# Decoder block with product-key experts on one core: every second weight block split by GpSimd, fewer activation pairs in routing and gate grid, and gate rows laid out with the routing

## The chip, the cores and the metric

One core of a Trainium2 chip runs the whole program. The metric is the device time of one execution in microseconds (us). Besides TensorE (matmul, PE in the profile, with PEld for its weight loads), VectorE (DVE), ScalarE (ACT) and GpSimd (POOL), the core has SyncE (SP), whose queue issues most of the loads. The profile shows TensorE's granted clock, where 1.00 is 2.4 GHz and 0.50 is 1.2 GHz.

## The reference, cut to what matters

The input x has 256 tokens of 1024 columns. A first half of the block (two attention branches, merged by gates) gives a new x. Then comes the expert layer, around which everything here turns:

```
h2 = modulate(rms_norm(x, g_ffn), sh2, sc2)
x = x + gt2 * peer_ffn(h2, w_pq, peer_keys, peer_u, peer_v)
return rms_norm(x, g_final)

peer_ffn, per token:
    q = h2 @ w_pq                                   # 8 heads x 2 halves x 128
    sub = q . peer_keys                             # 8 x 2 x 128 scores
    s_top, i_top = top_k(sub, 16)                   # per head and half
    best, pos = top_k(all 16 x 16 sums, 16)         # per head: 16 experts out of 16384
    gate = softmax(best)
    act = gelu(h2 . peer_u[expert])
    out = sum over experts of gate * act * peer_v[expert]
```

All matrices are float32. gt2 is one row of 1024 values, the last gate.

## The kernel before, in words

Nothing is gathered. The kernel computes the activations of all 16,384 experts for all 256 tokens, scatters the gates into a dense grid G (zero where an expert was not chosen), multiplies and sums over all experts. The experts are cut into 128 blocks of 128. A block of weights u (or v) is 128 x 1024 float32, 512 KB.

Each float32 product is made of three matmuls in a faster float type: `mm3` (L84 to L87) multiplies high by high, low by high and high by low parts. `unit` (L89) loads a block on SP's queue into a tile `raw`, and `split` (L80) makes the two parts: ScalarE copies raw to `hi` (L81), VectorE subtracts (L82) to get `lo`. The pool `stream` has four buffers each for raw, hi and lo.

The order of the stages:

- The first half of the block up to the query projection (0 to 294 us in the profile).
- `upair` (L574) computes the activations of two blocks j and j+1, 48 matmuls of 256 columns. `u_spill` (L582) puts gelu over it (L584) and stores the result in DRAM, `act_spill` (L585). Blocks 0 to J0 = 116 go this way, 58 pairs; the last six pairs are computed in the sum stage ("direct", tile `pum`).
- Routing (L643 to L722), for two tiles of 128 tokens: the subkey scores (`psub`, L650), the top 16 on VectorE (`top16`, L631: MAX8, FIND_INDEX8, MATCH_REPLACE8), the pair sums `cand`, their top 16, the two expert indices (`eq`, L701 to L705) and the softmax, turned into `selT` by three transposes (`psel`, L716).
- Gate grid (L742 to L758): for each of 64 groups of four tokens, VectorE compares selT with an iota (E and A, L746) and multiplies (two B, L753); `grid_mm` (L732) does 12 small bf16 matmuls per block (`pg`, L737; the profile shows two blocks together as 24), and ScalarE copies the result into G (L740). A has 2 buffers, B has 4, E has 1.
- Sum (L799 to L833): for each of 64 pairs, `act_of` (L778) loads the stored activations (`a`), `weighted` (L786) multiplies them by G on VectorE (L787) and splits the product (wh, wl); two blocks of v are loaded and split; 24 matmuls of 512 columns per pair add to four accumulators `acc`.
- At the end the last gate's row is multiplied with the sum, x is added, and the second norm is done.

Routing and grid are mostly VectorE's work, and pairs of `upair` are put between their steps: `u_some(share)` (L589) adds up shares and computes a pair for each whole one. The share of a step is a count written at the call, divided by PACE_R in the routing and PACE_G in the grid (L28, L29); a last `u_some(J0)` (L759) computes what is left. Per token tile the routing has shares of 4 (four times), 1, 3.8 (twice) and 5 (twice), over PACE_R; each grid block has 1 over PACE_G.

The compiler then orders each engine's instructions by their place in the program and by when it expects their inputs to be ready, places the buffers and writes all waits. On the chip each engine runs its instructions in that fixed order.

The gate row is laid out over all partitions in the sum stage, in the third last round (L808 to L824): for each of 8 groups of 128 columns VectorE multiplies the identity by a column of `mod` (`dg`, L822, two buffers), TensorE multiplies it by a tile of ones (`pgt`, L823; each is two passes in the profile), and VectorE copies four at a time to `gtb` (L824). In the same round g_final (L814) and x (`x1`, L816) are loaded.

Of the kernel before, what the change touches and what calls it, by code (L numbers as in the profile page):

```python
# [7 lines left out]
F32 = mybir.dt.float32  # L8
# [4 lines left out]
AF = mybir.ActivationFunctionType  # L13
OP = mybir.AluOpType
# [4 lines left out]
P = 128  # L19
T = 256  # L20
D = 1024
NC8 = D // P
# [2 lines left out]

J0 = 116

PACE_R = 2.5  # L28
PACE_G = 2.0  # L29

ON_PE = (0, 1, 2, 3)

# [2 lines left out]
def kernel(  # L35
# [24 lines left out]
    nc = tc.nc  # L60
# [5 lines left out]
    dpool = ctx.enter_context(tc.tile_pool(name="spill", bufs=1, space=DRAM))  # L66
    pp = ctx.enter_context(tc.tile_pool(name="pp", bufs=2, space=PSUM))

    act_spill = dpool.tile([J0 // 2, P, 2 * T], F32, name="act_spill")
    x1_spill = dpool.tile([2, P, D], F32, name="x1_spill")  # L70

    ident = cpool.tile([P, P], F32, name="ident")
    mod = cpool.tile([P, 48], F32, name="mod")
# [3 lines left out]

    last_split = []

    def split(hi, lo, src):  # L80
        nc.scalar.activation(hi, src, AF.Copy)  # L81
        last_split[:] = [nc.vector.tensor_sub(lo, src, hi.bitcast(F32))]  # L82

    def mm3(ps, lh, ll, rh, rl, start, stop):  # L84
        nc.tensor.matmul(ps, lh, rh, start=start, stop=False)  # L85
        nc.tensor.matmul(ps, lh, rl, start=False, stop=False)  # L86
        nc.tensor.matmul(ps, ll, rh, start=False, stop=stop)  # L87

    def unit(src, name, k=NC8, to=None):  # L89
        raw = stream.tile([P, D], F32, tag="raw", name=f"r_{name}")  # L90
        nc.sync.dma_start(raw, src)
        hi, lo = to or [stream.tile([P, D], F32R, tag=t, name=f"{t[0]}_{name}") for t in ("hi", "lo")]
        split(hi, lo, raw)
        return hi.rearrange("p (k n) -> p k n", k=k), lo.rearrange("p (k n) -> p k n", k=k)

    def rsqrt(r, m, q, n=1):
# [20 lines left out]
    neg_one = xpool.tile([P, P], F32, name="neg_one")  # L117
# [44 lines left out]
    def ada1(k):  # L162

        raw = spool.tile([P, 2, D], F32, tag="ada", bufs=3, name=f"ada1_{k}")
        nc.sync.dma_start(raw, w_ada[2 * k : 2 * k + 2].rearrange("k p d -> p k d"))
        got = []
        for i in range(2):
            t = 2 * k + i
            if t in ON_PE:
                row = pp.tile([1, P], F32, tag="pp", name=f"row_{t}")  # L170
                wk = raw[:, i].rearrange("p (k n) -> p k n", k=NC8)
                for j in range(NC8):
                    nc.tensor.matmul(row, cc[:, j : j + 1], wk[:, j], start=(j == 0), stop=(j == NC8 - 1))
                rs = spool.tile([1, P], F32, tag="rs", bufs=2, name=f"rs_{t}")
                nc.scalar.activation(rs, row, AF.Copy, scale=-1.0)
                cm = pm.tile([P, 1], F32, tag="mm", name=f"cm_{t}")
                nc.tensor.matmul(cm, rs, neg_one[0:1, 0:1], start=True, stop=True)
                got.append(cm)
            else:
                dots(raw[:, i : i + 1], t)  # L180
                got.append(mod[:, t : t + 1])
        g, b = gs[:, 0, k : k + 1], mod[:, 2 * k + 1 : 2 * k + 2]
        nc.vector.scalar_tensor_tensor(
            g, got[0], bcol1[:, k : k + 1], gcol[:, 0, k : k + 1], op0=OP.add, op1=OP.mult
        )
        nc.vector.tensor_add(b, got[1], bcol[:, 2 * k + 1 : 2 * k + 2])
        return g, b
# [74 lines left out]
    for k in range(NC8):  # L262
# [3 lines left out]
        g, b = ada1(k)  # L266
# [238 lines left out]
    for q in range(2):  # L505
        wd = unit(w_dil_o[q], f"dilo{q}", k=2)
        for r in range(2):
            ws = unit(w_sb_o[2 * q + r], f"sbo{q}{r}", k=4)
            br = []
            for nm, (wh, wl), kk, o0, c0 in (("s", ws, 4, 0, 0), ("d", wd, 2, 4, r * T)):  # L510
                ps = (pp if nm == "s" else pm).tile(
                    [P, 2, T], F32, tag="pp" if nm == "s" else "mm", name=f"br{nm}{q}{r}"
                )
# [6 lines left out]
            i = 4 * q + 2 * r  # L520
# [16 lines left out]
    for b in range(NC8):  # L537
        if b == NC8 - 1:
            ws = [unit(w_pq[m], f"pq0{m}") for m in range(2)]
        hi, lo = unit(w_out[b], f"out{b}")  # L540
        ps = pp.tile([P, T], F32, tag="pp", name=f"py{b}")
# [19 lines left out]
    for k in range(NC8):  # L561
        b = mod[:, 32 + k : 33 + k]
# [11 lines left out]
    def upair(j, name):  # L574
        ps = pp.tile([P, 2, T], F32, tag="pp", name=f"pu{name}")
        for s in range(2):
            hi, lo = unit(u[j + s], f"u{j + s}")
            for k in range(NC8):
                mm3(ps[:, s], hi[:, k], lo[:, k], hh[:, k], hl[:, k], k == 0, k == NC8 - 1)
        return ps  # L580
# [8 lines left out]
    def u_some(share):  # L589
        spilled[1] += share  # L590
        while spilled[1] >= 1.0 and spilled[0] < J0:
            u_spill(spilled[0])
            spilled[0] += 2
            spilled[1] -= 1.0
# [8 lines left out]
    rpool = es_r.enter_context(tc.tile_pool(name="route", bufs=1))  # L603
    pr_ = es_r.enter_context(tc.tile_pool(name="pr", bufs=3, space=PSUM))
    kT = rpool.tile([P, 16, P], F32, name="kT")
    nc.sync.dma_start(kT, keys.rearrange("p (a n) -> p a n", a=16))
    qT = rpool.tile([P, 16, T], F32, name="qT")
    ranks = rpool.tile([P, 16, P], BF16, name="ranks")
    pss = [pp.tile([P, T], F32, tag="pp", name=f"p_pq0{m}") for m in range(2)]
    for k in range(NC8):  # L610
# [4 lines left out]
    for b in range(1, 8):  # L615
        with tc.issue_after(h_made.ins if b == 1 else last_split[0].ins):
            ps = proj(2 * b, f"pq{b}", w_pq)
# [4 lines left out]
    for tt in range(2):  # L622
        xo = rpool.tile([P, NC8, P], F32, tag="xo", bufs=1, name=f"xo{tt}")
        for q in range(2):
            ps = pr_.tile([P, 4, P], F32, tag="t", name=f"px{tt}{q}")
# [17 lines left out]
    for tt in range(2):  # L643
# [3 lines left out]
        for q in range(4):  # L647
            ps = pr_.tile([P, 4, P], F32, tag="t", name=f"psub{tt}{q}")
            for i in range(4):
                nc.tensor.matmul(  # L650
                    ps[:, i], qT[:, 4 * q + i, P * tt : P * tt + P], kT[:, 4 * q + i], start=True, stop=True
                )
            sub = rpool.tile([P, 4, P], F32, tag="sub", bufs=2, name=f"sub{tt}{q}")
            copied = nc.scalar.activation(sub, ps, AF.Copy)
            if tt == 0 and q == 1:
                with tc.issue_after(copied.ins):
                    nc.scalar.activation(ranks, iota16[:, :, None].to_broadcast([P, 16, P]), AF.Copy)
            top16(s_top[:, 4 * q : 4 * q + 4], i_u[:, 4 * q : 4 * q + 4], sub, 4)
            u_some(4.0 / PACE_R)
        nc.vector.tensor_copy(i_top, i_u)  # L660


        cand = rpool.tile([P, 8, 112], F32, tag="cand", name=f"cand{tt}")
        st = s_top.rearrange("p (h x) k -> p h x k", x=2)
# [11 lines left out]
        )  # L676
        u_some(1.0 / PACE_R)
        for h in range(0, 8, 4):
            top16(best[:, h : h + 4], pos[:, h : h + 4], cand[:, h : h + 4], 4)
            u_some(3.8 / PACE_R)  # L680
        sel = rpool.tile([P, 3, 8, 16], F32, tag="sel", name=f"sel{tt}")
# [4 lines left out]
        for x, op, wide, narrow, off in (  # L686
# [18 lines left out]
            nc.vector.tensor_add(sel[:, x].rearrange("p h k -> p (h k)"), eq[:, 0], eq[:, 1])  # L705
            u_some(5.0 / PACE_R)
        ge = sel[:, 2]
# [6 lines left out]
        ps = pr_.tile([P, 3, P], F32, tag="t", name=f"psel{tt}")  # L714
# [27 lines left out]
    for b in range(T // 4):  # L742
# [14 lines left out]
        grid_mm(b, A, Bs)  # L757
        u_some(1.0 / PACE_G)  # L758
    u_some(J0)  # L759
# [5 lines left out]
    wpool = ctx.enter_context(tc.tile_pool(name="weighted", bufs=2))  # L765
# [35 lines left out]
    for n, j in enumerate(order):  # L801
        w = ws.pop(0)
        if n + 1 < n_pairs:
            ws.append(weighted(order[n + 1], acts.pop(0)))
        if n + 2 < n_pairs:
            acts.append(act_of(order[n + 2]))
        vs = [unit(vv[j + s], f"v{j + s}", k=1) for s in range(2)]
        if n == n_pairs - 3:  # L808
            gb = hpool.tile([P, 2, D], F32, tag="hh", name="gb")
            gtb, gfb = gb[:, 0], gb[:, 1]  # L810
            x1 = hpool.tile([P, 2, D], F32, tag="hl", name="x1")
            ones = wpool.tile([P, P], F32, name="ones")
            nc.vector.memset(ones, 1.0)
            nc.sync.dma_start(gfb, g_final.to_broadcast([P, D]))  # L814
            nc.scalar.activation(gfb, gfb, AF.Copy, scale=float(D**0.5))
            nc.sync.dma_start(x1, x1_spill.rearrange("a p d -> p a d"))  # L816
            for q in range(2):
                ps = pp.tile([P, 4, P], F32, tag="pp", name=f"pgt{q}")
                for k in range(4):
                    dg = wpool.tile([P, P], F32, tag="dg", name=f"dg{q}{k}")  # L820
                    i = 40 + 4 * q + k
                    nc.vector.tensor_scalar(dg, ident, mod[:, i : i + 1], None, op0=OP.mult)  # L822
                    nc.tensor.matmul(ps[:, k], ones, dg, start=True, stop=True)  # L823
                nc.vector.tensor_copy(gtb[:, 512 * q : 512 * q + 512], ps.rearrange("p a b -> p (a b)"))  # L824
        todo = [(w, vs)] if n < n_pairs - 1 else todo + [(w, vs)]
        if n < n_pairs - 2:
            for s in range(2):
                for b in range(4):
                    v_mm(s, b // 2, b % 2, w, vs[s], n == 0 and s == 0, False)
# [4 lines left out]

    st = wpool.tile([P, 2, 8], F32, tag="dg", name="st")

    def add_up(tt, e):
        cs_ = slice(512 * e, 512 * e + 512)  # L840
# [113 lines left out]
```

## Time and profile before

| what | value |
|---|---|
| median of 2 runs | 1099.66 us (1099.39 to 1099.94) |
| the profiled execution | 1100.67 us, its span in the profile 1098.9 us |
| TensorE matmul busy | 1063.5 us, 97% of the span |
| TensorE weight loads busy | 973.4 us, 89% (beside the matmuls) |
| VectorE busy | 832.3 us, 76% |
| ScalarE busy | 557.4 us, 51% |
| GpSimd busy | 0.2 us |
| loads and stores | 237.58 MB, mean 216 GB/s |

The span runs from the first to the last instruction of the profile; the execution's own time is 1.8 us longer. Durations of matmuls are modelled at their end and overlap, so the step from one start to the next tells what a matmul costs.

### The profile page before, as it was taken

How to read it: one execution, taken by the hardware profiler on the slowest of the kernel's cores; microseconds unless marked ns; L12 is line 12 of the kernel's file. 1: busy time of each engine (PE TensorE's matmuls, PEld its weight loads, DVE VectorE, ACT ScalarE, POOL GpSimd, SP SyncE). 2: the span in 40 equal slices, each digit the busy share in tenths (PEclk: the TensorE clock that was granted, in tenths of full speed). 3: DMA queues.
4: the chain of work that ended last, by engine and by line, in shares of the span. 5: the costliest groups of instructions: out<-in, count | busy, mean ns of one | idle time of the engine just before them, and what ended most of it. 6: DMA issues, size and time to landing. Idle time of an engine off the chain costs nothing.

```text
span 1098.9 us, 19552 instructions
## 1 busy us (share of the span) xinstructions
PE 1063.5 (97%) x7672; PEld 973.4 (89%) x7674; DVE 832.3 (76%) x1539; ACT 557.4 (51%) x706; POOL 0.2 (0%) x4
## 2 busy tenths in 40 slices
PE   7889999998999999999999999999999999999986
PEld 4878988998999999999999999888888888878865
DVE  6777886776799799778777787676777677677675
ACT  5496344655465545545454454544444444445432
POOL 0000000000000000000000000000000000000000
PEclk9999999999999999999999999999999999999998
DMA  9965567365866766755555555567676666668751
GB/s 334 370 222 177 185 230 266 105 211 210 297 220 221 244 206 198 246 181 189 175 191 175 183 183 182 190 216 253 212 249 225 235 220 239 221 222 276 255 195 39
DMA packets 74206, 237.58 MB, mean 216 GB/s; under 512 B 8449, under 2 KB 8833, under 8 KB 73986
## 3 DMA queue, kind: packets, MB, share of 16 engines
q1 hardware_dynamic: 64898, 220.04, 59.1%
q10 hardware_dynamic: 9216, 16.29, 4.0%
q8 instruction: 60, 0.98, 0.4%
q14 instruction: 32, 0.26, 0.1%
HBM read 219.00 MB, written 17.30 MB: 215 GB/s over the span
## 4 chain that ended last, share of the span: by engine, by line
PE 69%; DMA 8%; DVE 5%; issue 3%; ACT 1%; DVEq 0%; SPq 0%; ACTq 0%
PE pus L85 10%; PE pus L86 10%; PE pus L87 10%; PE acc L87 7%; PE acc L86 7%; PE acc L85 7%; DMA a<-act_spill 6%; PE pg L737 4%; DVE l_v L82 1%; DVE wl L82 1%; DMA r_pq<-in_w_pq_dram 1%; PE p_g L85 1%; PE p_g L86 1%; PE pum L87 1%; PE pum L85 1%
## 5 line engine op out<-in xcount | busy, mean ns | idle before, releaser
L85 PE MATMUL pus<-hh_n,h_u 128*128 128x256 f32 x928 | 265.7, 286 | 0.0
L86 PE MATMUL pus<-hl_n,h_u 128*128 128x256 f32 x928 | 262.6, 283 | 0.0
L87 PE MATMUL pus<-hh_n,l_u 128*128 128x256 f32 x928 | 262.4, 283 | 0.0
L81 ACT ACTIVATE h_u<-r_u 128x1024 fp32r<-128x1024 f32 x128 | 135.8, 1061 | 179.4 <-PE pus L86 151.1
L87 PE MATMUL acc<-h_v,wl 128*128 128x512 f32 x512 | 200.9, 393 | 1.0 <-DVE wl L82 0.6
L86 PE MATMUL acc<-l_v,wh 128*128 128x512 f32 x512 | 200.8, 392 | 0.6 <-DVE l_v L82 0.6
L85 PE MATMUL acc<-h_v,wh 128*128 128x512 f32 x512 | 200.1, 391 | 0.0
L81 ACT ACTIVATE h_v<-r_v 128x1024 fp32r<-128x1024 f32 x128 | 134.9, 1055 | 113.7 <-PE acc L87 56.5
L86 PEld LDWEIGHTS pus<-hl_n,h_u 128*128 128x128 f32 x928 | 178.0, 192 | 0.0
L87 PEld LDWEIGHTS pus<-hh_n,l_u 128*128 128x128 f32 x928 | 177.9, 192 | 0.0
L82 DVE TENSOR_TENSOR l_u<-r_u,h_u 128x1024 fp32r<-128x1024 f32 x128 | 155.1, 1219 | 30.1 <-ACT h_u L81 29.9
L85 PEld LDWEIGHTS pus<-hh_n,h_u 128*128 128x128 f32 x928 | 177.8, 192 | 0.0
L82 DVE TENSOR_TENSOR l_v<-r_v,h_v 128x1024 fp32r<-128x1024 f32 x128 | 154.2, 1220 | 15.2 <-ACT h_v L81 15.2
L787 DVE TENSOR_TENSOR a<-a,G 128x512 f32<-128x512 f32 x64 | 70.3, 1099 | 98.1 <-DMA a<-act_spill 98.1
L87 PEld LDWEIGHTS acc<-h_v,wl 128*128 128x128 f32 x512 | 96.5, 189 | 23.7 <-DVE wl L82 4.1
L86 PEld LDWEIGHTS acc<-l_v,wh 128*128 128x128 f32 x512 | 96.7, 189 | 21.6 <-DVE l_v L82 1.9
L85 PEld LDWEIGHTS acc<-h_v,wh 128*128 128x128 f32 x512 | 96.6, 189 | 19.7
L753 DVE TENSOR_TENSOR B<-E,selT 128x768 bf16<-128x768 bf16 x128 | 68.1, 552 | 33.1 <-PE pg L737 33.1
L81 ACT ACTIVATE wh<-a 128x512 fp32r<-128x512 f32 x64 | 40.4, 631 | 81.1 <-PE acc L86 74.8
L151 DVE SCALAR_TENSOR_TENSOR junk<-ada,c_sb 128x1024 bf16<-128x1024 f32 x44 | 53.6, 1218 | 2.8 <-DMA ada<-in_w_ada_dram 2.7
L737 PE MATMUL pg<-B,A 128*128 128x128 bf16 x768 | 52.0, 222 | 1.0 <-DVE rest L720 1.0
L737 PEld LDWEIGHTS <-A 128*128 128x128 bf16 x768 | 46.9, 114 | 2.5 <-issue 1.0
(319 smaller groups left out, 1809.4 us busy)
## 6 DMA issues: line engine op xcount, KB each, us to landing
r_u<-in_u_dram SPq DMA_DIRECT2D x128, 512.0 KB, 3.6
r_v<-in_v_dram SPq DMA_DIRECT2D x128, 512.0 KB, 4.4
ada<-in_w_ada_dram SPq DMA_DIRECT2D x20, 1024.0 KB, 7.4
act_spill<-as ACTq DMA_DIRECT2D x58, 256.0 KB, 2.3
a<-act_spill SPq DMA_DIRECT2D x58, 256.0 KB, 3.7
r_g<-in_w_in_dram SPq DMA_DIRECT2D x16, 512.0 KB, 4.0
r_pq<-in_w_pq_dram SPq DMA_DIRECT2D x16, 512.0 KB, 6.3
r_first<-in_w_in_dram SPq DMA_DIRECT2D x8, 512.0 KB, 7.1
```

Source lines behind the costliest of these rows:

```text
L81: nc.scalar.activation(hi, src, AF.Copy)
L82: last_split[:] = [nc.vector.tensor_sub(lo, src, hi.bitcast(F32))]
L85: nc.tensor.matmul(ps, lh, rh, start=start, stop=False)
L86: nc.tensor.matmul(ps, lh, rl, start=False, stop=False)
L87: nc.tensor.matmul(ps, ll, rh, start=False, stop=stop)
L151: nc.vector.scalar_tensor_tensor(junk, raw[:, k], 1.0, c_sb, op0=OP.mult, op1=OP.mult, accum_out=mod[:, t + k : t + k + 1])
L737: nc.tensor.matmul(ps[:, t], A[:, :, t], Bs[t // 2][:, x, :, t % 2], start=(x == 0), stop=(x == 2))
L753: nc.vector.tensor_tensor(B, E[:, None, :, 2 * q : 2 * q + 2].to_broadcast([P, 3, P, 2]), g, op=OP.mult)
L787: nc.vector.tensor_mul(a, a, G[:, :, j : j + 2].rearrange("p t s -> p s t"))
```

## The change: one split in two on GpSimd, other paces, gate rows earlier

`split` and `unit` get an argument for the engine that subtracts. In `upair`, the first of two blocks is split by VectorE as before and the second by GpSimd (ScalarE's copy stays). This holds for all 64 pairs of u, the direct ones too; no other split changes. PACE_R goes from 2.5 to 3.4 and PACE_G from 2.0 to 3.7. The gate row is laid out in a new function `gate_rows`, called in the routing after the subkey scores of the first token tile, with the tile `xo`, the routing's PSUM buffers and ScalarE for the copies; it is stored in DRAM as a third row of `x1_spill`, and loaded from there in the third last round of the sum, between g_final and x1. The constant -1 twice takes the place of the tile of ones.

```diff
-PACE_R = 2.5
-PACE_G = 2.0
+PACE_R = 3.4
+PACE_G = 3.7
...
-    x1_spill = dpool.tile([2, P, D], F32, name="x1_spill")
+    x1_spill = dpool.tile([3, P, D], F32, name="x1_spill")
...
-    def split(hi, lo, src):
+    def split(hi, lo, src, by=None):
         nc.scalar.activation(hi, src, AF.Copy)
-        last_split[:] = [nc.vector.tensor_sub(lo, src, hi.bitcast(F32))]
+        last_split[:] = [(by or nc.vector).tensor_sub(lo, src, hi.bitcast(F32))]
...
-    def unit(src, name, k=NC8, to=None):
+    def unit(src, name, k=NC8, to=None, by=None):
...
-        split(hi, lo, raw)
+        split(hi, lo, raw, by)
...
     def upair(j, name):
         ps = pp.tile([P, 2, T], F32, tag="pp", name=f"pu{name}")
         for s in range(2):
-            hi, lo = unit(u[j + s], f"u{j + s}")
+            hi, lo = unit(u[j + s], f"u{j + s}", by=(nc.vector, nc.gpsimd)[s])
...
+    def gate_rows():
+
+        go = rpool.tile([P, D], F32, tag="xo", bufs=1, name="go")
+        for q in range(2):
+            ps = pr_.tile([P, 4, P], F32, tag="t", name=f"pgt{q}")
+            for k in range(4):
+                dg = rpool.tile([P, P], F32, tag="dg", bufs=2, name=f"dg{q}{k}")
+                i = 40 + 4 * q + k
+                nc.vector.tensor_scalar(dg, ident, mod[:, i : i + 1], -1.0, op0=OP.mult, op1=OP.mult)
+                nc.tensor.matmul(ps[:, k], neg_one, dg, start=True, stop=True)
+            nc.scalar.activation(go[:, 512 * q : 512 * q + 512], ps.rearrange("p a b -> p (a b)"), AF.Copy)
+        nc.scalar.dma_start(x1_spill[2], go)
...
             u_some(4.0 / PACE_R)
+        if tt == 0:
+            gate_rows()
         nc.vector.tensor_copy(i_top, i_u)
...
-            ones = wpool.tile([P, P], F32, name="ones")
-            nc.vector.memset(ones, 1.0)
             nc.sync.dma_start(gfb, g_final.to_broadcast([P, D]))
             nc.scalar.activation(gfb, gfb, AF.Copy, scale=float(D**0.5))
-            nc.sync.dma_start(x1, x1_spill.rearrange("a p d -> p a d"))
-            for q in range(2):
-                ps = pp.tile([P, 4, P], F32, tag="pp", name=f"pgt{q}")
-                for k in range(4):
-                    dg = wpool.tile([P, P], F32, tag="dg", name=f"dg{q}{k}")
-                    i = 40 + 4 * q + k
-                    nc.vector.tensor_scalar(dg, ident, mod[:, i : i + 1], None, op0=OP.mult)
-                    nc.tensor.matmul(ps[:, k], ones, dg, start=True, stop=True)
-                nc.vector.tensor_copy(gtb[:, 512 * q : 512 * q + 512], ps.rearrange("p a b -> p (a b)"))
+            nc.sync.dma_start(gtb, x1_spill[2])
+            nc.sync.dma_start(x1, x1_spill[0:2].rearrange("a p d -> p a d"))
...
-    st = wpool.tile([P, 2, 8], F32, tag="dg", name="st")
+    st = wpool.tile([P, 2, 8], F32, name="st")
```

## Rows read from the trace of the kernel before

**Rows 1.** Busy time of each engine by stage: routing, change, grid, change, sum.
```profile
core 0: us, PE busy (x) PEld busy (x) DVE busy (x) ACT busy (x) POOL busy (x), PEclk, DMA share, GB/s
294.00:460.00 166.00, 165.93 (x1389) 165.73 (x1388) 150.15 (x520) 93.86 (x106) 0.00 (x0) 1.00 0.68 226
...
470.00:690.00 220.00, 220.00 (x2180) 218.67 (x2179) 174.06 (x302) 108.80 (x152) 0.00 (x0) 1.00 0.54 182
...
712.00:1063.00 351.00, 350.11 (x1625) 291.16 (x1625) 244.07 (x245) 168.90 (x191) 0.00 (x0) 1.00 0.70 235
```

**Rows 2.** Waits of TensorE from 294 to 1063 us: total, times, longest.
```profile
PE pg L737 <- DVE rest L720: 1.0, 1, 1.0
PE acc L87 <- DVE wl L82: 0.6, 1, 0.6
PE acc L86 <- DVE l_v L82: 0.6, 1, 0.6
```

**Rows 3.** TensorE in order of time in the grid: start, us, what.
```profile
602.63 0.28 PE L87 MATMUL pus<-hh_n,l_u 128*128 128x256 f32 x1
602.76 1.62 PE L737 MATMUL pg<-B,A 128*128 128x128 bf16 x24
604.18 0.36 PE L85 MATMUL pus<-hh_n,h_u 128*128 128x256 f32 x1
604.38 0.28 PE L86 MATMUL pus<-hl_n,h_u 128*128 128x256 f32 x1
...
609.89 0.28 PE L87 MATMUL pus<-hh_n,l_u 128*128 128x256 f32 x1
610.02 1.63 PE L737 MATMUL pg<-B,A 128*128 128x128 bf16 x24
```

**Rows 4.** Waits of all engines in the grid, 470 to 690 us, longest first.
```profile
ACT h_u L81 <- PE pus L86: 111.0, 61, 1.8
DVE B L753 <- PE pg L737: 32.0, 30, 1.1
```

**Rows 5.** TensorE in order of time at the end.
```profile
1063.06 0.60 PE L823 MATMUL pgt<-dg,ones 128*128 128x128 f32 x4
1063.42 0.48 PE L85 MATMUL acc<-h_v,wh 128*128 128x512 f32 x1
1068.77 0.80 PE L823 MATMUL pgt<-dg,ones 128*128 128x128 f32 x2 [4.87 <-DVE dg L822]
...
1072.35 0.63 PE L85 MATMUL acc<-h_v,wh 128*128 128x512 f32 x1
1072.78 0.63 PE L86 MATMUL acc<-l_v,wh 128*128 128x512 f32 x1
...
1087.67 0.39 PE L86 MATMUL acc<-l_v,wh 128*128 128x512 f32 x1
1087.90 0.39 PE L87 MATMUL acc<-h_v,wl 128*128 128x512 f32 x1
...
1089.26 0.39 PE L87 MATMUL acc<-h_v,wl 128*128 128x512 f32 x1
```

**Rows 6.** VectorE in order of time at the end.
```profile
1066.36 1.03 DVE L787 TENSOR_TENSOR a<-a,G 128x512 f32<-128x512 f32 x1 [1.68 <-DMA a<-act_spill]
1067.30 1.22 DVE L82 TENSOR_TENSOR l_v<-r_v,h_v 128x1024 fp32r<-128x1024 f32 x1
1068.43 0.28 DVE L822 TENSOR_SCALAR dg<-ident,mod 128x128 f32<-128x128 f32 x1
```

**Rows 7.** Busy time in three short stretches; columns as in rows 1.
```profile
1000.00:1020.00 20.00, 20.00 (x101) 16.98 (x100) 13.22 (x14) 10.81 (x13) 0.00 (x0) 1.00 0.92 319
...
1069.00:1075.00 6.00, 6.00 (x21) 5.01 (x21) 3.20 (x8) 0.00 (x0) 0.00 (x0) 0.56 0.01 1
```

**Rows 8.** SP's queue in order of time: the last load of the sum.
```profile
1064.70 0.33 SPq L91 DMA_DIRECT2D r_v<-in_v_dram  x1
```

**Rows 9.** DMA issues of the whole run: count, KB each, median us to landing.
```profile
r_v<-in_v_dram SPq DMA_DIRECT2D x128, 512.0 KB, 4.4
```

**Rows 10.** VectorE's groups in the grid, 470 to 690 us: busy, mean ns.
```profile
L82 DVE TENSOR_TENSOR l_u<-r_u,h_u 128x1024 fp32r<-128x1024 f32 x61 | 74.5, 1221 | 12.3 <-ACT h_u L81 12.3
L753 DVE TENSOR_TENSOR B<-E,selT 128x768 bf16<-128x768 bf16 x120 | 63.8, 552 | 32.0 <-PE pg L737 32.0
L746 DVE TENSOR_TENSOR E<-selT,iota 128x512 bf16<-128x512 bf16 x61 | 25.7, 421 | 1.1
L746 DVE TENSOR_TENSOR A<-selT,iota 128x512 bf16<-128x512 bf16 x60 | 25.1, 418 | 0.0
```

**Rows 11.** VectorE's largest group in the routing, 300 to 460 us.
```profile
L82 DVE TENSOR_TENSOR l_u<-r_u,h_u 128x1024 fp32r<-128x1024 f32 x56 | 67.2, 1217 | 14.5 <-ACT h_u L81 14.3
```

**Rows 12.** Groups of the whole run on ScalarE and TensorE: busy, mean ns.
```profile
L81 ACT ACTIVATE h_u<-r_u 128x1024 fp32r<-128x1024 f32 x128 | 135.8, 1061 | 179.4 <-PE pus L86 151.1 <-DMA r_u<-in_u_dram 8.9 <-DVE cand L637 3.6
...
L584 ACT ACTIVATE as<-pus 128x512 f32<-128x512 f32 x58 | 33.8, 583 | 10.4 <-DMA act_spill<-as 6.5 <-PE pus L87 3.9
...
L650 PE MATMUL psub<-kT,qT 128*128 128x128 f32 x64 | 8.4, 275 | 0.0
```

**Rows 13.** All of GpSimd's groups, of which one stands here for four.
```profile
L944 POOL MEMSET const-float32-1.0<- 128x1 f32 x1 | 0.1, 100 | 0.0
```

## The prediction

> **What bounds the kernel now.** I began with the busy time by stage [rows 1]. The three long stretches that the change touches, routing (294 to 460 us), gate grid (470 to 690) and the sum over expert values (712 to 1063), have TensorE busy 165.9 of 166, 220.0 of 220 and 350.1 of 351 us at a granted clock of 1.00. VectorE is busy for 150 of 166 and 174 of 220. A busy TensorE can still hide waits, so the next view was who TensorE waited for from 294 to 1063: 2.2 us in three waits [rows 2]. Then its order of time in the grid [rows 3]: from one group of 24 small matmuls (two grid blocks) to the next, 602.76 to 610.02, 7.26 us pass. The small ones take 1.42 (602.76 to 604.18, 0.059 each), the 48 of a pair of weight blocks follow one another every 0.12 us (604.38 starts the second, 609.89 the last), 5.76 per pair. 1.42 + 5.76 = 7.18, so 0.08 is lost per period. VectorE is the one that waits there: its product B waits 32.0 us for TensorE to give buffers back, and ScalarE's copy h_u 111.0 [rows 4]. So up to 1063 TensorE sets the time, its matmuls stay the same in number, and relief for VectorE alone buys nothing.
>
> The tail is different. TensorE stands still for 4.9 us before the matmul that lays out gate rows, because the diagonal dg comes late from VectorE [rows 5]: dg at 1068.43 stands in VectorE's order behind a, which waited 1.68 us for a DMA, and behind l_v [rows 6]. After this stop the granted clock is 0.56 from 1069 to 1075 [rows 7], which is mostly the lower of the two levels (1.2 instead of 2.4 GHz): the acc matmuls are 0.43 apart instead of 0.227 (1072.35 and 1072.78 against 1087.67 and 1087.90) [rows 5].
>
> **The change part by part.**
>
> *Gate rows moved.* At 1063.06, where the first pgt starts, the three last pairs (72 acc matmuls) are open; the last starts at 1089.26 and takes a step of 0.227 [rows 5]. Without pgt they need 72 x 0.227 = 16.3 us and would end at 1079.4 instead of 1089.5: 10.1 us. This holds the stop, the low clock and the 16 pgt passes, four of which take 0.36 us (1063.06 to 1063.42). Those return in the routing, where TensorE has no gap: 16 x 0.09 = 1.4. What is late next: the last weight blocks r_v are asked for at 1064.70 [rows 8] and land 4.4 us later, the median of all such loads [rows 9]; with 1.06 for ScalarE's copy and 1.22 for VectorE's subtraction [rows 6, 12] the low part of the last one is there near 1071.5. TensorE reaches it after pair 61 and some ten matmuls, 1063.06 + 34 x 0.227 = 1070.8. I charge 1.0 for that, bounds 0 and 3. The tail behind the last matmul does not change.
>
> The new load of 512 KB sits on SP's queue between the loads of g_final and x1. All wait for the same two freed tiles, and behind them on that queue come a and r_v. From 1000 to 1020 us the DMA engines are busy 0.92 of the time at 319 GB/s [rows 7], so 0.52 MB is 1.6 us of them. TensorE was still busy 20.0 of 20 there, but the product of a and G waits for its DMA anyhow. Between 0 and 1.6 I take 0.5. In the routing the part adds eight dg of 0.28 us [rows 6], 2.2 us of VectorE, two ScalarE copies and one 512 KB store on ScalarE's queue, with no wait behind a busy buffer, since the x1 stores are long done.
> Net: 10.1 - 1.4 - 1.0 - 0.5 = 7.2 us less.
>
> *Fewer pairs between routing and grid.* A token tile hands out 4 x 4 + 1 + 2 x 3.8 + 2 x 5 = 34.6 shares in the routing, both 69.2, which was 27.7 pairs at 2.5 and is 20.4 at 3.4. The grid's 64 blocks gave 32 and give 17.3. So 20.4 of the 58 stored pairs are left for a stretch of their own behind the grid. There TensorE needs 5.76 us a pair, ScalarE two copies of 1.06 and one gelu of 0.58 [rows 12], VectorE one split. No cost, the same matmuls at the same step. TensorE's cover for the two other stages:
> - Grid: one block costs VectorE (174.06 - 74.5)/60 = 1.66 us [rows 1, 10]. After: 64 x 1.66 + 17.3 x 1.22 = 127 us of VectorE beside 64 x 0.71 + 17.3 x 5.76 = 145 of TensorE. Slack 18 us, against 46 in the rows of before.
> - Routing: VectorE's own work is 150.15 less 56 splits (67.2) less a few grid products (about 4), 79 us [rows 1, 11]. After: 79 + 20.4 x 1.22 + 2.2 = 106 against 20.4 x 5.76 = 118 plus 8 for the subkey matmuls [rows 12]. Slack 20 us.
> Both stay with TensorE. Fewer switches between small and large matmuls save at most 15 x 0.08 = 1.2 us; more, if blocks come singly, would cost as much. I take zero.
>
> *GpSimd's split.* Takes 64 subtractions of 1.22 us [rows 10] from VectorE, 78 us, of which none was on the path. The trace has no tile operation of GpSimd at all, only four memsets of one column at 0.1 us [rows 13]. Below I bound one split by VectorE's 1.22 us; from above, 5.76 us, one per pair, beyond which GpSimd itself would set the pace. I take 2.4, twice the nearest row. Its length alone costs nothing: four buffers let ScalarE start a block when the one four earlier is done, which leaves three blocks, 3 x 2.88 = 8.6 us, for 1.06 + 2.4 (even 1.06 + 5.76 fits). What it does to VectorE beside it is the open price: between 0 and a full stop of VectorE for as long as the split runs. In the grid the full stop is 17.3 x 1.22 = 21 us more of VectorE's time at the low end, 17.3 x 2.4 = 42 at my value and 100 at the high end; less the slack of 18 that is 3, 24 and 82 us. I take zero, the near end, because no row shows the two engines hinder each other and a split of VectorE keeps its length whatever runs beside it: the mean of l_u is 1217 ns in the routing and 1221 in the grid [rows 10, 11].
>
> The Trainium skill speaks against that. Its page "SBUF — State Buffer", section "SBUF: two separate sides", says that a VectorE instruction with two SBUF inputs and a GpSimd instruction that reads SBUF exclude one another for the whole instruction. In the grid all of VectorE's products have two SBUF inputs, so by that rule the full stop holds; no run here shows it yet. For the length, "GPSIMD Engine Reference", section "Performance versus the Vector engine", has 4497 ns for 2048 columns against 2293 on VectorE; half of it, about 2.25 us, is an estimate from that page.
>
> *Sum.* 1100.67 (the profiled execution) - 7.2 = 1093.5. The median shown is 1.0 lower than that execution, so 1092.5.
>
> **Rivals.**
> 1. *VectorE stands while GpSimd splits* (the far end above). For: the grid's slack falls from 46 to 18 us, and VectorE has next to no other wait there than TensorE's. Against: no row shows it. Price 24 us at a split of 2.4 us, the point of decision being a split of 18/17.3 = 1.0 us; 1093 + 24 gives about 1116, from 1098 (split of 1.3) up. This is the case that ends slower than before.
> 2. *The grid runs dry between pairs.* A has two buffers and B four, so VectorE is at most two blocks ahead. With 3 or 4 blocks in a row the third can start only when the first is multiplied. A and two Bs, some 1.3 us of the block's 1.66, come after that, beside 0.71 of TensorE for the second block: a gap of 0.6 at the third block, and 0.9 at the fourth (1.66 - 0.71). About 1.2 us per pair, 21 us in 17.3, gives 1113. Against: the compiler orders instructions by readiness and can put matmuls of the next pair between blocks.
> 3. *The late dg moves along.* In the routing VectorE is as busy as in the tail, dg again has two buffers, and TensorE waits in order. Another 5 us stop with its low clock (2 to 3 us) gives back the 7: 1100. Against: no DMA stands ahead of it on VectorE there, and TensorE's subkey matmuls wait for nothing longer than 1.0 us [rows 2].
>
> **How the numbers follow.** Forecast 0.50, rival 1 0.30, rival 2 0.08, rival 3 0.06, rivals 1 and 2 together (1122 and above) 0.06. The range runs from 1087 (no charge for late loads, switches saved, and some microseconds elsewhere) to 1118, which takes in rival 1 at its middle price; the forecast alone has 1088 to 1098. What a measurement tells from no change is about 2%, 22 us: faster than 1078 needs a gain that no stretch of TensorE offers (0.02), slower than 1122 needs rivals 1 and 2 together or a split beyond 2.8 us that stops VectorE (0.09), the rest 0.89.
>
> **What would show it.** Right: pgt gone from the tail and the last three pairs in about 17 us at a clock of 1.00; no wait of TensorE on VectorE above 1 us in grid and routing; l_u and B at 1.22 and 0.55 us; some 117 us of pure pair matmuls before the acc stage. Wrong: B, A or E longer than 0.42 to 0.55, or TensorE idle before pg with VectorE as releaser (rivals 1 and 2, told apart by those durations); TensorE waiting for dg in the routing (rival 3); GpSimd's split over 5.8 us.

## The result and the profile after

The changed kernel takes 1165.01 us in the median (1161.94 to 1168.08), against 1099.66 before: 1.0594 times as long, 95% interval 1.0474 to 1.0715. Forecast were 1092.5 us, range 1087 to 1118. The profiled execution took 1168.08 us, with a span of 1166.3.

Busy time by stage in the changed kernel, with the columns of [rows 1]; its stages end at other times (routing, grid, pairs alone, sum):

```profile
294.00:455.00 161.00, 144.12 (x1158) 142.74 (x1157) 128.36 (x499) 81.15 (x94) 73.47 (x22) 0.95 0.57 194
455.00:640.00 185.00, 151.73 (x1484) 146.98 (x1483) 156.98 (x256) 74.62 (x109) 38.71 (x16) 0.94 0.34 116
640.00:777.00 137.00, 137.00 (x1155) 136.96 (x1154) 33.25 (x31) 62.47 (x74) 52.64 (x22) 1.00 0.65 218
...
790.00:1141.00 351.00, 350.32 (x1630) 292.13 (x1629) 243.89 (x242) 169.57 (x193) 10.57 (x4) 1.00 0.70 236
```

TensorE has gaps in routing and grid now, 17 and 33 us, and a granted clock of 0.95 and 0.94 where [rows 1] had 1.00. The other two stages are full. Who it waited for, over the whole run, longest first; it answers to [rows 2]:

```profile
PE pg L752 <- DVE B L768: 33.3, 16, 2.1
PE pus L87 <- POOL l_u L82: 5.5, 1, 5.5
...
PE pgt L617 <- DVE dg L616: 4.1, 1, 4.1
PE pus L87 <- DVE l_u L82: 3.8, 1, 3.8
PE pg L752 <- DVE rest L735: 3.0, 1, 3.0
```

The first row is 16 waits of 2.1 us, one for nearly each pair in the grid. One of them on VectorE, in order of time:

```profile
542.57 0.42 DVE L761 TENSOR_TENSOR A<-selT,iota 128x512 bf16<-128x512 bf16 x1
542.90 2.71 DVE L768 TENSOR_TENSOR B<-E,selT 128x768 bf16<-128x768 bf16 x1
545.54 0.41 DVE L761 TENSOR_TENSOR A<-selT,iota 128x512 bf16<-128x512 bf16 x1
```

on GpSimd:

```profile
542.78 2.42 POOL L82 TENSOR_TENSOR l_u<-r_u,h_u 128x1024 fp32r<-128x1024 f32 x1 [8.79 <-ACT h_u L81]
```

and on TensorE:

```profile
541.51 2.08 PE L752 MATMUL pg<-B,A 128*128 128x128 bf16 x30
545.67 0.52 PE L752 MATMUL pg<-B,A 128*128 128x128 bf16 x6 [2.08 <-DVE B L768]
...
547.20 0.41 PE L86 MATMUL pus<-hl_n,h_u 128*128 128x256 f32 x1
547.41 0.41 PE L87 MATMUL pus<-hh_n,l_u 128*128 128x256 f32 x1
```

GpSimd starts at 542.78 and is done at 545.20. The product B that starts at 542.90 ends 0.41 us after that, and takes 2.71 instead of 0.55. TensorE stands for 2.08 us. From 546.56 on its matmuls are 0.21 us apart instead of 0.12 for some 3 us: the granted clock has gone to its lower level, as in the tail of before [rows 5, 7]. This followed six of the 16 stops and not the other ten. Two stops, ending near 523.2 and 534.4, lie in the first of these stretches, which keeps its 1.00; the second is the low stretch just shown:

```profile
516.00:546.00 30.00, 23.77 (x257) 22.88 (x255) 25.55 (x40) 13.22 (x19) 7.26 (x3) 1.00 0.34 115
546.60:549.90 3.30, 3.30 (x17) 3.30 (x17) 2.86 (x7) 0.22 (x1) 0.00 (x0) 0.50 0.37 143
```

The groups of the whole run, to hold against [rows 10, 13] (VectorE, GpSimd; busy, mean ns):

```profile
L768 DVE TENSOR_TENSOR B<-E,selT 128x768 bf16<-128x768 bf16 x128 | 101.6, 823 | 16.4 <-PE pg L752 15.4
...
L82 POOL TENSOR_TENSOR l_u<-r_u,h_u 128x1024 fp32r<-128x1024 f32 x64 | 175.4, 2742 | 894.3 <-ACT h_u L81 894.2
```

GpSimd's mean of 2742 ns hides two things: a median of 2404, near the 2.4 I had taken, and a longest of 13202. That one lies in the routing:

```profile
349.48 15.59 POOL L82 TENSOR_TENSOR l_u<-r_u,h_u 128x1024 fp32r<-128x1024 f32 x2 [2.80 <-ACT h_u L81]
```

Beside it VectorE, which had begun a two-input product at 349.36, goes from one such product to the next without a pause, until an operation with one input comes at 360.40:

```profile
359.26 1.21 DVE L82 TENSOR_TENSOR l_u<-r_u,h_u 128x1024 fp32r<-128x1024 f32 x1
360.40 0.27 DVE L726 TENSOR_REDUCE gsum<-sel 128x8 f32<-128x128 f32 x1
360.70 0.20 DVE L727 RECIPROCAL gsum<-gsum 128x8 f32<-128x8 f32 x1
360.94 1.88 DVE L728 TENSOR_TENSOR sel<-sel,gsum 128x128 f32<-128x128 f32 x1
```

Here GpSimd is the one kept out: the first split is done at about 362.7 (349.48 + 13.2), the length of one split after the reduce, and the product at 360.94 waits for it in turn. TensorE waits 5.5 us for that low part, the row with POOL above.

To compare runs I count, per stage, the time from the first matmul of its kind to the first of the next, and what its matmuls need at the steps of [rows 3, 5] (0.12, 0.059 and 0.227 us; 0.1 for the few others). The rest is "lost" (some records of small matmuls are missing, so it is good to 2 us or so).

| kernel (pace routing / grid, who splits) | routing, lost | grid, lost | sum stage, lost | ratio to before, 95% |
|---|---|---|---|---|
| before (2.5 / 2.0, VectorE) | 166.7, 2.4 | 222.1, 1.8 | 385.4, 12.8 | |
| changed (3.4 / 3.7, GpSimd) | 151.3, 25.5 | 191.1, 52.4 | 378.5, 7.4 | 1.0594 [1.0474, 1.0715] |
| e1 (3.4 / 3.7, VectorE, gate rows moved) | 138.5, 12.3 | 147.9, 7.5 | 378.2, 7.2 | 1.008 [1.006, 1.010] |
| e2 (2.5 / 2.0, GpSimd) | 176.5, 12.0 | 226.6, 4.1 | 384.5, 11.8 | 1.016 [1.0112, 1.0209] |
| e3 (2.5 / 2.0, VectorE, gate rows moved) | 170.2, 3.5 | 222.1, 4.3 | 375.9, 4.9 | 0.9946 [0.9927, 0.9966] |
| e4 (3.4 / 3.7, VectorE) | 138.4, 13.8 | 148.0, 9.9 | 385.7, 13.0 | 1.0143 [1.0095, 1.0191] |
| f1 (3.4 / 2.0, GpSimd, moved) | 150.0, 24.3 | 223.1, 1.4 | 376.8, 5.8 | 1.0148 [1.0102, 1.0194] |
| f2 (2.5 / 3.7, GpSimd, moved) | 181.5, 15.3 | 191.9, 51.4 | 377.3, 6.3 | 1.0526 [1.0486, 1.0567] |

From before to the changed kernel that is +23 in the routing, +51 in the grid and -5 in the sum. The stretch of pairs alone between grid and sum, 134.0 us in the changed kernel, loses 0.1, where the 13.9 us of before lost 2.3. Together that is 66, nearly all of the 67 that lie between the two spans (1166.3 and 1098.9).

### The profile page after: what moved, and what is told of

Its sections match the earlier page's. It is cut to its first block, busy times and chain, and to the rows that moved or that the text cites. A ratio compares the mean times of both kernels' runs of the same rounds, so it can differ in the third digit from the quotient of the medians.

```text
span 1166.3 us, 19545 instructions
## 1 busy us (share of the span) xinstructions
PE 1083.6 (93%) x7672; PEld 989.4 (85%) x7674; DVE 809.0 (69%) x1472; ACT 560.9 (48%) x708; POOL 175.6 (15%) x68
## 4 chain that ended last, share of the span: by engine, by line
PE 57%; DVE 15%; DMA 9%; issue 3%; ACT 2%; POOL 2%; DVEq 0%; SPq 0%; ACTq 0%; POOLq 0%
PE pus L85 8%; PE pus L87 8%; PE pus L86 8%; PE acc L87 7%; PE acc L86 7%; PE acc L85 7%; DVE B L768 5%; DMA a<-act_spill 4%; PE pg L752 3%; POOL l_u L82 2%; DMA ada<-in_w_ada_dram 1%; DVE l_u L82 1%; DVE wl L82 1%; DVE l_v L82 1%; PE p_g L85 1%
## 5 line engine op out<-in xcount | busy, mean ns | idle before, releaser
L82 POOL TENSOR_TENSOR l_u<-r_u,h_u 128x1024 fp32r<-128x1024 f32 x64 | 175.4, 2742 | 894.3 <-ACT h_u L81 894.2
L87 PE MATMUL pus<-hh_n,l_u 128*128 128x256 f32 x928 | 269.0, 290 | 9.4 <-POOL l_u L82 5.5
L85 PE MATMUL pus<-hh_n,h_u 128*128 128x256 f32 x928 | 272.2, 293 | 0.4 <-ACT as L584 0.4
L86 PE MATMUL pus<-hl_n,h_u 128*128 128x256 f32 x928 | 268.4, 289 | 0.0
L87 PEld LDWEIGHTS pus<-hh_n,l_u 128*128 128x128 f32 x928 | 184.1, 198 | 10.1 <-POOL l_u L82 5.8
L85 PEld LDWEIGHTS pus<-hh_n,h_u 128*128 128x128 f32 x928 | 184.2, 198 | 0.7 <-ACT as L584 0.7
L86 PEld LDWEIGHTS pus<-hl_n,h_u 128*128 128x128 f32 x928 | 184.3, 199 | 0.0
L82 DVE TENSOR_TENSOR l_u<-r_u,h_u 128x1024 fp32r<-128x1024 f32 x64 | 83.5, 1305 | 130.9 <-ACT h_u L81 130.9
L768 DVE TENSOR_TENSOR B<-E,selT 128x768 bf16<-128x768 bf16 x128 | 101.6, 823 | 16.4 <-PE pg L752 15.4
L752 PE MATMUL pg<-B,A 128*128 128x128 bf16 x768 | 58.5, 228 | 36.2 <-DVE B L768 33.3
```

The costliest lines, as they stand in the source:

```text
L82: last_split[:] = [(by or nc.vector).tensor_sub(lo, src, hi.bitcast(F32))]
L752: nc.tensor.matmul(ps[:, t], A[:, :, t], Bs[t // 2][:, x, :, t % 2], start=(x == 0), stop=(x == 2))
L768: nc.vector.tensor_tensor(B, E[:, None, :, 2 * q : 2 * q + 2].to_broadcast([P, 3, P, 2]), g, op=OP.mult)
```

## The experiments

**One part at a time.** e1 takes GpSimd out of the changed kernel:

```diff
-            hi, lo = unit(u[j + s], f"u{j + s}", by=(nc.vector, nc.gpsimd)[s])
+            hi, lo = unit(u[j + s], f"u{j + s}")
```

> The changed kernel with the second block of a pair split by VectorE again (paces and gate rows stay changed). Theory A (GpSimd's split and VectorE's two-input products stop one another): the loss goes, 1090 to 1102 us, B back at about 552 ns, no wait of TensorE for B above 1 us. Theory B (the grid runs dry at 3.7 blocks per pair because VectorE is only two blocks ahead): the loss stays for the most part, 1115 to 1165 us, with waits of pg for B of 0.6 to 2 us at B of 552 ns. Theory C (the late dg in the routing with its low clock): 4 to 7 us of loss stay at one place, whatever A and B do.

Measured 1.008. The 33 us of waits for B are gone and B is back at 553 ns. Theory B falls: no wait of pg for B stands among TensorE's. The grid still loses 7.5 us, which no wait of TensorE names; I did not follow that further. A new wait of 4.6 us in three places is for VectorE's l_u, in the routing. The wait for dg that theory C names stands there too, 2.5 us at one place. The time, 1111.73 us, is above theory A's range, because the paces cost something of their own (e4).

e2 is the kernel before with GpSimd's split alone (the edit above, reversed, with the argument `by`):

> The kernel before with GpSimd's split alone (paces 2.5 and 2.0, gate rows at the end). Theory A: slower than before; each of some 30 pairs in the grid stops VectorE for one split of 2.4 us, but VectorE has 2.7 us of idle time per period of 7.26 once it is rid of one split, so between 0 and 2 us per pair: 1100 to 1160 us, B above 650 ns on average. Theory B: 1100 us within 5, since the paces are those of before.

Measured 1.016. This told most about the interplay. Busy time of the grid (columns of [rows 1]) and the group of B:

```profile
480.00:700.00 220.00, 220.00 (x2180) 218.71 (x2180) 206.93 (x276) 110.06 (x152) 74.07 (x30) 1.00 0.56 182
```
```profile
L753 DVE TENSOR_TENSOR B<-E,selT 128x768 bf16<-128x768 bf16 x128 | 136.9, 1090 | 12.4 <-PE pg L737 11.3
```

VectorE is stopped more often than in the changed kernel, B takes 1090 ns in the mean. Yet TensorE is busy 220 of 220: VectorE's busy time in this stretch rose from 172 us in before to 207, and there was room for it. Only at the grid's last block, at 705.15, one stop of 2.1 us comes through. Theory B, no change, is refuted. What e2 loses lies in the routing, nearly half of it in one wait of 5.6 us for GpSimd's low part, and the tail of before is still there.

e3 is the gate rows alone (the changed kernel with both paces and the split taken back):

> The kernel before with the gate rows laid out in the routing, nothing else. My sum for this part: 7 us less, 1089 to 1095 us, with no wait for dg in the tail. Theory C: the 4 us wait for dg and its low clock appear in the routing, and 1097 to 1101 us are left.

Measured 0.9946, about 6 us less. The last three pairs take 18.2 us from their first matmul to the end of the last, where before had 26.1 and my sum 16.3 with 1.0 for late loads. A wait for dg of 1.9 us stands in the routing, the moved stop of theory C at less than half its size.

e4 is the paces alone:

```diff
-PACE_R = 2.5
-PACE_G = 2.0
+PACE_R = 3.4
+PACE_G = 3.7
```

> The kernel before with the paces 3.4 and 3.7 alone. VectorE does all splits, so the grid has 64 x 1.66 + 17.3 x 2.44 = 148 us of VectorE beside 145 of TensorE. Theory A: 1098 to 1108 us. Theory B: 1115 to 1140 us, with waits of pg for B.

Measured 1.0143, 1118.35 us. That lies in theory B's range, but not by its mechanism: TensorE never waits for B here. Neither theory has the reason. The loss is 11 us more in the routing and 8 in the grid. In the routing four waits of TensorE, 8.8 us in total, are for VectorE's l_u; two on TensorE in order of time:

```profile
338.39 0.39 PE L87 MATMUL pus<-hh_n,l_u 128*128 128x256 f32 x1 [1.96 <-DVE l_u L82]
...
343.87 0.58 PE L87 MATMUL pus<-hh_n,l_u 128*128 128x256 f32 x1 [2.35 <-DVE l_u L82]
```

VectorE issues that l_u at 342.59, behind a whole round of top-16 operations, 20 short ones in 4.3 us, that begins at 338.25. With fewer pairs per step, TensorE comes to the next pair before VectorE comes to its split.

**How the parts work together.** f1 and f2 take back one pace each:

> The changed kernel with the grid's pace back at 2.0 (pace 3.4 in the routing, GpSimd's split and gate rows stay). Theory A2 (GpSimd's split stops VectorE for 2.4 us per pair at any pace, but TensorE feels it only where VectorE has no slack: 2.7 us per period at pace 2.0, none at 3.7): TensorE's lost time in the grid falls from 52 us to 10 or less, 1112 to 1126 us, while B stays above 700 ns on average. Rival (each split costs TensorE 2.4 us whatever the pace): about 25 pairs of stops instead of 16, 1170 us or more.

> The changed kernel with the routing's pace back at 2.5 (3.7 in the grid, GpSimd's split and gate rows stay). Theory A2: the routing's lost time falls from 25 us to about 12, as with GpSimd's split alone; the grid keeps its stops of 2.4 us for 16 pairs: 1145 to 1160 us. Rival (the routing's loss is GpSimd being kept out, and the pace is nothing): 1160 to 1168 us.

Measured 1.0148 and 1.0526. The group of B in f1 and then in f2, and between them f1's grid (columns of [rows 1]):

```profile
L768 DVE TENSOR_TENSOR B<-E,selT 128x768 bf16<-128x768 bf16 x128 | 134.6, 1073 | 12.2 <-PE pg L752 11.0
```
```profile
455.00:670.00 215.00, 215.00 (x2138) 213.71 (x2138) 201.94 (x267) 107.33 (x150) 72.63 (x30) 1.00 0.55 180
```
```profile
L768 DVE TENSOR_TENSOR B<-E,selT 128x768 bf16<-128x768 bf16 x128 | 101.7, 824 | 16.2 <-PE pg L752 15.3
```

In f1 30 of the products B are stopped and the grid loses 1.4 us; in f2 16 are stopped and it loses 51.4. So the stop of VectorE has no price of its own. It costs TensorE nothing where VectorE has slack at that place, and nearly all of it where three blocks stand in a row (36 small matmuls, 541.51 above). The routing loses 24.3 at pace 3.4 and 15.3 at 2.5, so both the pace and GpSimd count there.

**What stops what.** f3 lets GpSimd only write, f4 lets it read one tile. Both leave out the true low part of every second block of u:

```diff
         nc.scalar.activation(hi, src, AF.Copy)
-        last_split[:] = [(by or nc.vector).tensor_sub(lo, src, hi.bitcast(F32))]
+        if by is nc.gpsimd:
+            last_split[:] = [nc.gpsimd.memset(lo.bitcast(F32), 0.0)]
+        else:
+            last_split[:] = [nc.vector.tensor_sub(lo, src, hi.bitcast(F32))]
```

(f4 has `nc.gpsimd.tensor_copy(lo, src)` in the place of the memset.)

> The changed kernel in which GpSimd fills the low part of every second block with zero instead of subtracting, so that it only writes (the low part of half of the blocks of u is left out). If the stop comes from GpSimd reading beside a VectorE product with two inputs: B back at about 552 ns, no wait of TensorE for B above 1 us, 1100 to 1115 us. Rival (any work of GpSimd on the shared memory stops VectorE): B above 600 ns and waits for B in the grid of about the length of the fill.

> The changed kernel in which GpSimd copies raw to the low part instead of subtracting, so that it reads one tile instead of two (the low part of half of the blocks of u is wrong by that). Reading is what stops: B is stretched by the length of the copy, about half to all of 2.4 us, and the time lies between the write-only run and the changed kernel, 1110 to 1160 us. Rival (only two reads at once stop VectorE): B at about 552 ns and the time of the write-only run.

Measured 0.9993 [0.9973, 1.0013] and 1.0153 [1.0117, 1.0189]. In f3 a fill of 0.98 us lies across a product B without touching it. That happens 16 times in the run, and no B takes more than 0.56 us. On GpSimd and then on VectorE:

```profile
502.35 0.98 POOL L83 MEMSET l_u<- 128x1024 f32 x1 [8.08 <-PE pus L90]
```
```profile
502.66 0.56 DVE L771 TENSOR_TENSOR B<-E,selT 128x768 bf16<-128x768 bf16 x1 [0.88 <-PE pg L755]
```

In f4 a copy of 1.05 us stops B until it is done (499.95), again 16 times, with 1.15 to 1.21 us for each of these B. On GpSimd and then on VectorE:

```profile
498.90 1.05 POOL L83 CAST l_u<-r_u 128x1024 fp32r<-128x1024 f32 x1 [8.60 <-PE pus L90]
```
```profile
499.21 1.15 DVE L771 TENSOR_TENSOR B<-E,selT 128x768 bf16<-128x768 bf16 x1 [0.87 <-PE pg L755]
```

So it is GpSimd's reading that excludes a VectorE product with two inputs, and one tile read is enough. The grid loses 5.9 us in f3 and 15.7 in f4. The profile puts 15 of TensorE's 16 waits in f4's grid, 0.5 us each, down to ScalarE's copy into G. But at every one of the 16 the A that stands right behind the stopped B on VectorE ends 0.06 us before the matmul, so I read them as the same stop. f4's copy doesn't wait for ScalarE's half and so starts at other times; its size compares with the split's only roughly.

g3 halves GpSimd's share and leaves the other 512 columns to VectorE:

```diff
+            nc.gpsimd.tensor_sub(lo[:, 0:512], src[:, 0:512], hi[:, 0:512].bitcast(F32))
+            last_split[:] = [nc.vector.tensor_sub(lo[:, 512:D], src[:, 512:D], hi[:, 512:D].bitcast(F32))]
```

> The changed kernel with GpSimd subtracting only half of the columns of every second block and VectorE the other half. If the stop lasts as long as GpSimd's instruction: it is about 1.2 us instead of 2.4, so TensorE waits about 1 us per pair in the grid instead of 2.4, and the time lies in the middle between the changed kernel and the one with VectorE's splits, 1120 to 1145 us. Rival (a fixed cost per instruction of GpSimd): near the changed kernel, 1150 us or more.

Measured 1.0286 [1.0264, 1.0308], 1134 us, in the middle as the first line said. GpSimd's half and the B beside it:

```profile
523.57 1.34 POOL L83 TENSOR_TENSOR l_u<-r_u,h_u 128x512 fp32r<-128x512 f32 x1 [8.79 <-ACT h_u L81]
```
```profile
523.69 1.64 DVE L772 TENSOR_TENSOR B<-E,selT 128x768 bf16<-128x768 bf16 x1
```

TensorE waits 16 times 1.0 us, so the wait follows the length of GpSimd's instruction. The grid loses 23.9 us, and its granted clock is 1.00: none of these shorter stops was followed by the lower level.

**A version that is faster than both.** g0 is e3 once more, g1 lays the gate rows out ahead of the routing, g2 lets GpSimd make dg at the place of e3 (both with eight buffers):

```diff
-                dg = rpool.tile([P, P], F32, tag="dg", bufs=2, name=f"dg{q}{k}")
+                dg = rpool.tile([P, P], F32, tag="dg", bufs=8, name=f"dg{q}{k}")
...
-                nc.vector.tensor_scalar(dg, ident, mod[:, i : i + 1], -1.0, op0=OP.mult, op1=OP.mult)
+                nc.gpsimd.tensor_scalar(dg, ident, mod[:, i : i + 1], -1.0, op0=OP.mult, op1=OP.mult)
```

> The kernel before with the gate rows laid out in the routing, once more, as the measure for the next two on the same chip: 0.993 to 0.997 of before, about 1096 us, with one wait of about 2 us for dg in the routing.

> As the run before, but the gate rows are laid out ahead of the routing's first step, with eight buffers for dg, where VectorE has idle time. If the 2 us wait for dg (rival 3 of the prediction) is what is left of the gate rows' cost: the wait goes and 1 to 3 us are gained on the run before, 1093 to 1095 us. Rival (the wait only moves to another late product of VectorE): no change.

> As the first run, but GpSimd makes the eight diagonals dg, with eight buffers, so that they stand in no queue of VectorE. One input each, 128 columns: they are short, and VectorE mostly runs one-input operations there, so neither stops the other for long: the wait for dg goes, 1093 to 1095 us. Rival (GpSimd's work there stops VectorE's split and TensorE waits for that): 1096 us or more.

Measured 0.9935 [0.9918, 0.9952], 0.9927 [0.9906, 0.9947] and 0.9918 [0.9902, 0.9935]. The wait for dg, 2.4 us in g0, is gone in g1 and g2. In g1 a wait of 2.5 us for wl stands at the start of the sum. It is 0.8 in g0 but 1.9 in e3, which is the same kernel, so it isn't shown that the wait only moved there, as g1's rival has it. g2 has the lowest median, 1092.81 us, but its interval overlaps g0's: shown is that these three beat before by 6 to 9 us, not the order among them.

## Why the prediction was wrong

1. *The step that failed* is in "GpSimd's split": "I take zero, the near end, because no row shows the two engines hinder each other". No row of before could show it, since GpSimd had no tile operation there [rows 13]; the absence of rows was taken for a reason. The equal means of l_u in routing and grid don't speak for it either, since no GpSimd work lay beside them. In its place: a split of GpSimd and a two-input product of VectorE exclude each other, so a B that meets a split takes 2.71 us instead of 0.55. The cause is GpSimd's reading (f3, f4), and the stop is as long as GpSimd's instruction (g3). The rule of the Trainium skill, "SBUF — State Buffer", "SBUF: two separate sides", which the prediction cited and set aside, agrees with these runs: reading beside two inputs excludes, writing alone does not, and the one that comes second stands still. The length estimated from the Trainium skill's "GPSIMD Engine Reference", "Performance versus the Vector engine", 2.25 us, compares with a median of 2.40 measured.
2. *The price of rival 1 was set too low.* I had set the stops of a whole stage against the slack of a whole stage, 42 - 18 = 24 us. The grid lost 51 more. The order of instructions is fixed before the run, for a VectorE that nobody stops; at the place of the stop the third block of a row was due at once, so 2.1 of 2.4 us came through 16 times, 33 us. The low clock in the grid (0.94 over 185 us) took some 10 us more, an estimate from that share. The rest, some 8, comes with the pace: e1, e4 and f3 lose 5.9 to 9.9 us in the grid, against 1.8 in before, without a wait for B and at a clock of 1.00, spread over many short steps between small matmuls; why is open. f1 shows the other end: stops of the same length, slack at the place, nothing lost. A slack is worth what stands where the stop falls.
3. *The routing was priced at no loss* ("slack 20 us"). It lost 23 more. Some 11 come from the pace (e4): the average leaves room, but VectorE works off a round of 20 short operations before the next split. Some 10 come from GpSimd (e2), nearly half of it in one split that was itself kept out, which I had not thought of. Only the 4 us for dg was among the rivals (rival 3).
4. *Rival 2*, the grid running dry for 21 us, fell in e1 and e4: no wait for B without GpSimd's reads, and a grid that loses under 10 us. The compiler had put matmuls of the pairs between the blocks, as written against it: in the changed kernel 36 small ones, then some of a pair, then 12.
5. *The gate rows* were right in mechanism and near in size: forecast 7.2 us, e3 gave 6.0 (1102.41 x 0.0054). The tail itself gained 7.9 us (26.1 to 18.2), and the wait for dg, 1.9 us in e3 and 4.1 in the changed kernel, took part of it back.
6. The pairs alone at the end cost nothing, as forecast.

## What to carry to other kernels

Before work moves to GpSimd, look at what VectorE runs beside it: in these runs a GpSimd instruction that reads tiles and a VectorE instruction with two inputs excluded each other (2.71 us for a B of 0.55), so moved work of 1.2 us can take 2.4 us from the engine it was to relieve. Average slack of a stage doesn't pay for a stop; ask which instruction is due at the place where it falls, above all where the order was fixed for engines that don't stop. And where one engine is full without gaps, relief for another can't gain anything, while what makes the full one wait costs the wait and can cost its clock behind it.

## What the runs showed of the hardware that was not expected

- A run of two-input products without a pause on VectorE kept one GpSimd split out for about 11 us of 13.2, until a reduce with one input came. MAX8, FIND_INDEX8 and MATCH_REPLACE8 aren't stopped: the 74 of them that lie inside a split of the changed kernel take 271 to 277 ns in the mean of each kind, where before has 270 to 279.
- After six of the 16 stops of 2.1 us in the grid TensorE's matmuls came at half rate for some 3 us (granted clock 0.50 from 546.6 to 549.9); over the grid the granted clock was 0.94. After the 16 stops of 1.0 us in g3 it stayed at 1.00.
- GpSimd needs 2.40 us for the subtraction of 128 x 1024, 1.05 for a copy, 0.96 for a fill (f3), and 0.37 for a product of 128 x 128 with one tile (g2), each as long as nothing keeps it out.
